# A layer kernel with RWKV-7, band attention and memory attention on one core: the odd chunks of a triangular inverse laid crosswise over TensorE, and three numbers of its planner changed

## The chip, the core and the metric

The kernel runs on one core of a Trainium2 chip. The metric is the device time of one execution in microseconds. A change of less than 0.2% (5.4 us) is about what a measurement of this kernel cannot tell from no change.

TensorE (PE in the profile) multiplies, VectorE (DVE) and ScalarE (ACT) do the elementwise work and empty PSUM, GpSimd (POOL) makes a reduction over partitions for each weight tile, and SyncE (SP) issues the DMA transfers. A weight load of TensorE stands as PEld.

## The reference

Two layers over 512 tokens with 1024 channels. Each layer is a half-step FFN, a mixing block with three branches, and a second half-step FFN:

```python
x = x + 0.5 * swiglu(rms_norm(x, norm_ffn1[l]), ffn1_w_in[l], ffn1_w_out[l])
h = rms_norm(x, norm_mix[l])
proj = h @ w_in[l]            # RWKV | band attention | memory attention
y_rwkv, y_att, y_mem = rwkv7_time_mix(...), chunked_rel_attention(...), memory_attention(...)
merged = g_rwkv * (y_rwkv @ w_branch_rwkv[l]) + g_att * (y_att @ w_branch_att[l]) + g_mem * (y_mem @ w_branch_mem[l])
x = x + merged @ w_out[l]
x = x + 0.5 * swiglu(rms_norm(x, norm_ffn2[l]), ffn2_w_in[l], ffn2_w_out[l])
```

The part that is changed is in the RWKV branch, a scan over time with 8 heads of 64 channels:

```python
def step(state, inp):
    r_t, w_t, k_t, v_t, kk_t, b_t = inp
    sa = jnp.einsum('bhvk,bhk->bhv', state, kk_t)
    state = state * w_t[:, :, None, :] - sa[..., None] * b_t[:, :, None, :] + v_t[..., None] * k_t[:, :, None, :]
    return state, jnp.einsum('bhvk,bhk->bhv', state, r_t)
```

## The kernel before

**Two kinds of products.** The large products (FFN, projections, gates, branches, output) run in fp16: every weight tile comes from HBM as float32 (`wr`), is split by ACT and DVE into a high and a low half (`wh`), and each product is three fp16 products of 128 rows by 128 columns by 512 tokens (`hh`, `hl`, `ab`, `ya`, `ym`, `yr` against `wh`; tiles `g` and `as` in PSUM). RWKV and the two attentions compute in float32 with small products.

**The scan in chunks.** The 512 steps are cut into 8 chunks of 64. `rwkv` runs over four pairs `p` of heads; the two heads of a pair lie on partitions 0 to 63 and 64 to 127 (`H2`; `W2` is the same pair the other way round). For each pair it makes decays and scaled keys (`ar`, `be`, `ka`), then per half of the chunks one block of 16 products `be` and `ka` against `ar`, 64 by 64 by 128 (the "be/ka blocks" below): `be` goes from a head's partitions to the other head's columns, `ka` to its own, so the four 64 by 64 quarters of TensorE are all used. DVE masks the result into `gx` and `g1`.

**The inverse.** The unit lower triangular 64 by 64 matrix of each chunk and head is inverted by doubling. `lab` holds the matrix, `tt` the transposed inverse so far, `ti` the inverse so far. Level 0 needs no product. Levels 1 to 4 (`for n in range(1, 5)`) each take a mask product on DVE (`lm`), a block of 16 products `lm` by `tt` (`each`; rows `s<-tt,ta` in the trace), a copy of it to `p1` (tile `ka`) on ACT, a second block of 16 products `ti` by `p1` (rows `s<-ka,ti`), a subtraction from `tt` on DVE, and four transposes with four copies that refresh `ti` (`turned`, `placed`; the list `PL` says S or V for each copy). There are 2 layers x 4 pairs x 4 levels x 2 = 64 such blocks. A last level works on 32 by 32 pieces. In `each` before, head 0 goes from rows 0 to 63 to columns 0 to 63 and head 1 from rows 64 to 127 to columns 64 to 127: two of the four quarters are used. A float32 product stands in the trace as two instructions, so a block of 16 has 32.

**After the inverse** the 8 chunks go one after the other: `xps`, `cx`, `vu`, the state `vz`, and the output `yp`.

**What sets the order.** No engine's order is written by hand. `Plan` records every operation with its dependencies; a block (`plan.block()`) is one operation of TensorE. `run` then builds a list schedule with costs in us (`cost`, `GROUPS`, `HOPS`), and each engine issues in the order of that plan (every instruction has the line of the replay, L560 before and L562 after). An operation's priority is its `tail`, the longest path behind it, plus a `lift`. Four rules of `run` matter here:

- `GROUPS` gives the cost of a block by number and shape of its products. Where it has no entry, the costs of the single products are added: a be/ka block is then 16 x (0.0255 + 128 / 1200) = 2.1 us.
- `RATIO, DEBT`: each float32 operation adds 0.45 of its cost to a debt, each fp16 operation takes its cost off. Where the debt is over `DEBT`, a float32 operation that would be next has to let an fp16 product go first.
- A pool's tile of a tag waits until all users of the tile that had the buffer are done. Tag `s` in PSUM has two buffers, tag `ta` in SBUF has one.
- `WARM`: where TensorE would wait for over 0.4 us in the plan, the wait is filled with products of a zero tile (`xps<-wt`, 320 columns), which nothing uses.

The fp16 products that can stand between the small ones are the projections (until all are made) and then gates and branches; a gate may run ahead of its branch by two tiles only.

Of the kernel before, what the change touches and what calls it, by code (L numbers as in the profile page):

```python
# [10 lines left out]
AF = mybir.ActivationFunctionType  # L11
ALU = mybir.AluOpType
# [4 lines left out]
P = 128  # L17
# [12 lines left out]
EXPC = 0.6065306597126334  # L30
SPREAD = 3
FIRSTS = ("x00", "pv0", "con", "x01", "w1")
LIFT = 110
PCS = [[0], [1, 2, 3]]
FIRST = 2
# [192 lines left out]
class Plan:  # L228
# [1 line left out]
    GROUPS = {  # L230
        2: {(128, CH, CH): 0.266, (CH, CH, CH): 0.264, **{(CH, P, n): 0.212 + n * 0.001656 for n in (128, 256, 384, 512)}},
        4: {(128, CH, CH): 0.5},
        16: {(CH, CH, CH): 1.08},
    }
    HOPS = {"PE": (0.2, 0.2), "S": (0.14, 0.27), "V": (0.14, 0.21), "G": (0.06, 0.3), "D": (0.5, 0.5)}
    SLACK = 0.04
    RATIO, DEBT = 0.45, 0.5

    def __init__(self, tc):
        nc = tc.nc  # L240
# [337 lines left out]
def trunk(tc: tile.TileContext, i: dict, out: bass.AP, dbg: dict | None = None, depth: int = DEPTH):  # L578
# [32 lines left out]
    def as_stream(name, f, *a):  # L611
        old, stream[0] = stream[0], name
        r = f(*a)
        stream[0] = old
        return r
# [10 lines left out]
    def s_ps():  # L626
        return pq.tile([P, T], F32, tag="s", name=nm("s"))
# [290 lines left out]
    def chunk(src, k=KT):  # L918
        w, d = load_w(src, src.shape[-1])
        return w.rearrange("p s (k n) -> p s k n", k=k), d  # L920
# [72 lines left out]
    def mixing(l, pieces, kst):  # L993
# [43 lines left out]
        def project():  # L1037
            lw = tr("lw")
            D.dma_start(out=lw, in_=i["lora"][l, 0])
            gw = tr("gw")  # L1040
            D.dma_start(out=gw, in_=i["lora"][l, 1])
            w, d = chunk(i["w_in"][l, 0])
            dd = mul_d(d, d_h)
            ps = [g_ps(), g_ps()]
            for c0, c1 in HV:
                mm3x2([x[:, c0:c1] for x in ps], [([(w[:, 0, k, u * P:(u + 1) * P], w[:, 1, k, u * P:(u + 1) * P]) for u in range(2)], hh[:, k, c0:c1], hl[:, k, c0:c1]) for k in range(KT)])
            plan.phase += 1
            xwa = shift(ps[0], dd, 12, "xwa")
            S.activation(xwa[0:CH, :], xwa[0:CH, :], AF.Tanh)
            xg = shift(ps[1], dd, 13, "xg")  # L1050
            S.activation(xg, xg, AF.Tanh, scale=0.5)
            V.tensor_scalar(out=xg, in0=xg, scalar1=0.5, scalar2=0.5, op0=ALU.mult, op1=ALU.add)
            glob.update(lw=lw, gw=gw, xwa=xwa, xg=xg)
            if l > 0:
                va, dva = chunk(i["vres_a"])
                vb = tr("vb", [32, T])
                D.dma_start(out=vb, in_=i["vres_b"])
                ps = g_ps()
                mm3(ps[0:32, :], [(va[:, 0, k, :], va[:, 1, k, :], hh[:, k, :], hl[:, k, :]) for k in range(KT)])
                dv = mul_d(dva, d_h)  # L1060
                hv = tm("yr", bufs=5)[0:32, :]
                S.activation(hv, ps[0:32, :], AF.Copy, scale=dv[0:32, 0:1])
                glob.update(vb=vb, hv=hv)
            for x, p in PLAN:
                if x == "rkv":
                    w, d = chunk(i["w_in"][l, 1 + p])
                    dd = mul_d(d, d_h)
                    r_ = shift(lin(w, d, 0, hh, hl), dd, p, "r")
                    k_ = shift(lin(w, d, 1, hh, hl), dd, 4 + p, "k")
                    w, d = chunk(i["w_v"][l, p])  # L1070
                    rkv_of[p] = r_, k_, shift(lin(w, d, 0, hh, hl), mul_d(d, d_h), 8 + p, "v")
                elif x == "att":
                    w, d = chunk(i["w_av"][l, p])
                    dd = mul_d(d, d_h)
                    ps = g_ps()
                    for b in range(4):
                        mm3(ps[:, b * P:(b + 1) * P], [(hh[:, k, b * P:(b + 1) * P], hl[:, k, b * P:(b + 1) * P], w[:, 0, k, :], w[:, 1, k, :]) for k in range(KT)])
                    vt = ta_("vt", [P, 4, P], bufs=2)
                    S.activation(vt, ps.rearrange("p (b n) -> p b n", b=4), AF.Copy, scale=dd[:, 0:1])
                    V.tensor_reduce(out=vm[:, p:p + 1], in_=vt, op=ALU.max, axis=AX.XY, apply_absolute_value=True)  # L1080
                    w, d = chunk(i["w_in"][l, 5 + p])
                    dd = mul_d(d, d_h)
                    qk = []
                    for u in range(2):
                        t = ta_("ak" if u else "aq", bufs=2)
                        S.activation(t, lin(w, d, u, hh, hl), AF.Copy, scale=dd[:, 0:1])
                        qk.append(t)
                    att_of[p] = qk[0], qk[1], vt
                else:
                    w, d = chunk(i["w_in"][l, 9 + p])  # L1090
                    dd = mul_d(d, d_h)
                    for u in range(2):
                        t = ta_("ak" if u else "aq", bufs=2)
                        S.activation(t, lin(w, d, u, hh, hl), AF.Copy, scale=dd[:, 0:1])
                        mq_of[2 * p + u] = t
# [3 lines left out]

        def band():  # L1100
            for p in range(NP):
                q_, k_, vt = att_of[p]
                bias = ta_("bias", [P, 2, 2 * P])
                D.dma_start(out=bias, in_=i["bias"][l, p])
# [77 lines left out]
        def mem_att():  # L1182
            for c in range(2):
                for u in range(2):
                    j = 2 * c + u
                    q_ = mq_of[j]
                    sq = ta_("sc", bufs=3)
                    S.activation(sq, q_, AF.Square)
# [42 lines left out]
        def c8(t):  # L1231
            return t.rearrange("p (c s) -> p c s", c=NCH)

        def lev(c0, n=NCH):
            return con[:, c0:c0 + CH].unsqueeze(1).to_broadcast([P, n, CH])

        def each(ps, f, to=H2):
            with plan.block():
                for c in range(NCH):
                    for h, o in zip(H2, to):  # L1240
                        a, b = f(h, c)
                        PE.matmul(ps[o, c * CH:(c + 1) * CH], lhsT=a, rhs=b, start=True, stop=True)

        def turned(src):

            ps = s_ps()
            with plan.block():
                for b in range(4):
                    PE.transpose(ps[:, b * P:(b + 1) * P], src[:, b * P:(b + 1) * P], ident)
            return ps.rearrange("p (b h a) -> p b h a", b=4, h=2)  # L1250

        def placed(ps, dst, engines):

            for n, (r, h) in enumerate(((0, 0), (1, 1), (0, 1), (1, 0))):
                o = dst(h).rearrange("p (b r) a -> p b r a", r=2)[:, :, r, :]
                if engines[n] == "S":
                    S.activation(o, ps[H2[r], :, h, :], AF.Copy)
                else:
                    V.tensor_copy(o, ps[H2[r], :, h, :])
# [2 lines left out]

        def rwkv():
            for p in range(NP):
                cs = slice(p * P, (p + 1) * P)
                r_, k_, v_ = rkv_of[p]

# [75 lines left out]
                placed(turned(ut.rearrange("p c s -> p (c s)")), lambda h: lab[H2[h]], PL[20:24])  # L1343
                V.tensor_tensor(out=tt, in0=ut, in1=lev(C_LEV1T), op=ALU.mult)
                V.tensor_tensor(out=tt, in0=lev(C_EYE), in1=tt, op=ALU.subtract)
                ti = tr("ti", [P, NCH, CH])
                V.tensor_tensor(out=ti, in0=lab, in1=lev(C_LEV), op=ALU.mult)
                V.tensor_tensor(out=ti, in0=lev(C_EYE), in1=ti, op=ALU.subtract)
                aw = small("aw", 8)
                for u, h in enumerate(H2):  # L1350
                    o, x = gx[W2[u], :, u, :], ar[h].rearrange("p c a s -> p c (a s)")
# [14 lines left out]
                for n in range(1, 5):  # L1366
                    lm = tr("ta", [P, NCH, CH])
                    V.tensor_tensor(out=lm, in0=lab, in1=lev(C_LEV + n * CH), op=ALU.mult)
                    ps = s_ps()
                    each(ps, lambda h, c: (lm[h, c, :], tt[h, c, :]))  # L1370
                    p1 = tr("ka", [P, NCH, CH])
                    S.activation(p1, c8(ps), AF.Copy)
                    pt = s_ps()
                    each(pt, lambda h, c: (ti[h, c, :], p1[h, c, :]))
                    V.tensor_tensor(out=tt, in0=tt, in1=c8(pt), op=ALU.subtract)
                    placed(turned(tt.rearrange("p c s -> p (c s)")), lambda h: ti[H2[h]], PL[16:20])

                up, low = [[slice(CH * h + b, CH * h + b + CH // 2) for h in range(2)] for b in (0, CH // 2)]
                lo, hi = slice(0, CH // 2), slice(CH // 2, CH)
# [95 lines left out]

        def branch(b, y):
            for m in range(4):
                w, d = chunk(i["w_gate"][l, b * 4 + m])
                dg = mul_d(d, d_h, 0.5)
                bw, bd = chunk(i["w_branch"][l, b, m], k=4)  # L1480
# [21 lines left out]
                        S.activation(sq, acc[n], AF.Square, accum_out=qm[:, n:n + 1])  # L1502

        as_stream("f", project)
        plan.lift = LIFT
        as_stream("m", rwkv)
        plan.lift = 0.0
        as_stream("a", band)
        as_stream("a", mem_att)
        tst.close()  # L1510
        gp = tst.enter_context(plan.pool(name=nm("gp"), bufs=1, reuse_waits="tile"))
        acc.extend(gp.tile([P, T], F32, name=nm("acc")) for _ in range(4))
# [3 lines left out]
        for b, y in ((1, ya), (2, ym), (0, yr)):  # L1516
            wide[0] = b != 1
            as_stream("f", branch, b, y)
        plan.step(False)
        dump(f"acc{l}", acc[0])  # L1520

# [182 lines left out]
```

## Time and profile before

| | |
|---|---|
| median of 3 runs | 2720.83 us (2719.52 to 2721.28) |
| profiled execution | 2720.14 us |
| its span, first to last instruction | 2718.4 us |
| busy | PE 2682.8, PEld 1458.5, DVE 1623.0, ACT 1534.9, POOL 111.9 us |
| mean granted clock of TensorE | 0.997 |
| read from HBM | 239.09 MB, 91 GB/s with the writes over the span |

The trace falls into five stretches: the first FFN (0 to 400 us), the mixing of layer 0 (400 to 884), two FFNs (884 to 1768), the mixing of layer 1 (1768 to 2244), and the last FFN. RWKV, the attentions and everything that the change touches lie in the two mixing stretches.

How to read the rows: a timeline row has the start in us from the span's start, the length in us, the engine, the line, the operation, the tiles written and read, the array's shape (`64*64`), the size and the number of instructions merged; in brackets the idle time of the engine before it and what ended it. A matmul's own length includes its way through the array, so what it costs is the distance to the next start. A row of a stretch gives per engine the busy us and in brackets the instructions, and then TensorE's granted clock, the DMA share and GB/s. A row of a group gives the count, and behind the bar the busy us, the mean ns of one, and the idle us before them.

### The profile page before, as it was taken

Reading aid. Unit: us, or ns where it says so; the run is one execution under the profiler, and the core shown is the slowest. Engines: PE = TensorE matmul, PEld = TensorE weight load, DVE = VectorE, ACT = ScalarE, POOL = GpSimd, SP = SyncE. Lnnn points to the kernel's source line nnn. Section 1 sums busy time; section 2 is a strip of 40 time slices with the busy share of each in tenths; the row PEclk is TensorE's granted clock in tenths of the full one; section 3 lists DMA queues with packets and bytes.
Section 4 is the critical chain, followed back from the end, with each engine's and each line's share of the span. In section 5 each row is a group of like instructions: output and inputs, shape, how many; then the busy total and the mean of one; then the engine's idle time right before and its main releaser. Section 6 shows DMA issues by size and latency. Waiting matters only on the chain.

```text
span 2718.4 us, 45525 instructions
## 1 busy us (share of the span) xinstructions
PE 2682.8 (99%) x18206; PEld 1458.5 (54%) x18206; DVE 1623.0 (60%) x4391; ACT 1534.9 (56%) x2543; POOL 111.9 (4%) x285
## 2 busy tenths in 40 slices
PE   9999999999999999999999999999999999999999
PEld 6444486565645465444564444765645454654445
DVE  6345487788676675354463444777876756743543
ACT  6556465665545666565455654665655546655652
POOL 0000000000000000000000000000000000000000
PEclk9999999999999999999999999999999999999999
DMA  5222342121121223222222223311102213223232
GB/s 172 102 100 105 113 144 75 63 71 36 47 86 71 93 94 118 108 99 97 99 109 99 104 101 124 120 68 59 63 28 78 74 48 113 94 105 106 96 109 78
DMA packets 47158, 249.37 MB, mean 92 GB/s; under 512 B 5312, under 2 KB 10688, under 8 KB 23648
## 3 DMA queue, kind: packets, MB, share of 16 engines
q1 hardware_dynamic: 46944, 246.45, 25.6%
q8 instruction: 143, 2.34, 0.3%
q14 instruction: 71, 0.58, 0.1%
HBM read 239.09 MB, written 7.34 MB: 91 GB/s over the span
## 4 chain that ended last, share of the span: by engine, by line
PE 87%; DVE 8%; ACT 2%; issue 1%; DMA 0%; POOL 0%; SPq 0%; ACTq 0%; POOLq 0%; DVEq 0%
PE g L560 45%; PE as L560 33%; PE s L560 5%; PE xps L560 3%; DVE wh L560 1%; DVE w L560 1%; PE yp L560 1%; DVE gx L560 1%; DVE rs L560 1%; DVE sc L560 1%; ACT wh L560 0%; DVE ar L560 0%; ACT pt L560 0%; DVE tt L560 0%; DVE be L560 0%
## 5 line engine op out<-in xcount | busy, mean ns | idle before, releaser
L560 PEld LDWEIGHTS <-wh 128*128 128x128 f16 x10920 | 1049.8, 98 | 1017.0 <-issue 31.6
L560 PE MATMUL g<-hh,wh 128*128 128x512 f16 (+1 forms) x3216 | 984.2, 367 | 3.0 <-DVE r L560 2.1
L560 ACT ACTIVATE wh<-wr,qs 128x1024 f16<-128x1024 f32 (+2 forms) x478 | 482.9, 1050 | 222.4 <-PE g L560 120.4
L560 ACT ACTIVATE junk<-wr 128x2048 uint8<-128x2048 f32 (+2 forms) x239 | 413.0, 1728 | 333.3 <-DMA wr<-ffn_in 142.4
L560 PE MATMUL g<-hl,wh 128*128 128x512 f16 (+1 forms) x1608 | 589.2, 366 | 0.0
L560 DVE SCALAR_TENSOR_TENSOR wh<-wr,qs,wh 128x1024 f16<-128x1024 f32 (+2 forms) x478 | 544.4, 1169 | 48.6 <-ACT wh L560 47.7
L560 PE MATMUL as<-hh,wh 128*128 128x512 f16 (+1 forms) x1536 | 443.4, 361 | 0.0
L560 PE MATMUL as<-hl,wh 128*128 128x512 f16 (+1 forms) x768 | 277.4, 361 | 0.0
L560 PE MATMUL as<-ab,wh 128*128 128x512 f16 (+1 forms) x1224 | 234.7, 350 | 0.0
L560 PE MATMUL g<-ab,wh 128*128 128x512 f16 (+1 forms) x1224 | 234.5, 350 | 0.0
L560 POOL PARTITION_ALL_REDUCE ar<-wm x239 | 97.4, 408 | 2391.9 <-ACT junk L560 2171.0
L560 DVE SCALAR_TENSOR_TENSOR a<-g,md,sg 128x512 f32<-128x512 f32 x44 | 33.0, 751 | 213.5 <-PE g L560 209.3
L560 DVE SCALAR_TENSOR_TENSOR a<-as,md,sg 128x512 f32<-128x512 f32 x44 | 33.0, 751 | 213.3 <-PE as L560 210.1
L560 DVE SCALAR_TENSOR_TENSOR x<-g,md,x 128x512 f32<-128x512 f32 (+1 forms) x62 | 39.0, 629 | 116.2 <-PE g L560 116.1
L560 DVE SCALAR_TENSOR_TENSOR x<-as,md,x 128x512 f32<-128x512 f32 (+1 forms) x62 | 39.0, 629 | 114.6 <-PE as L560 114.6
L560 DVE TENSOR_SCALAR qt<-ar 128x1 int32<-128x1 int32 x253 | 37.9, 151 | 103.1 <-POOL ar L560 100.8
L560 ACT ACTIVATE sq<-x 128x256 f32<-128x256 f32 x96 | 37.0, 407 | 79.5 <-DVE x L560 51.9
L560 PE MATMUL xps<-wt 128*128 128x320 f16 x390 | 64.0, 312 | 5.1 <-DVE ta L560 3.8
L560 DVE SCALAR_TENSOR_TENSOR ab<-a,qs,ab 128x512 f16<-128x512 f32 x88 | 60.7, 747 | 9.6 <-ACT ab L560 9.3
L560 ACT ACTIVATE ti<-s 64x256 f32<-64x256 f32 (+1 forms) x144 | 54.3, 377 | 17.9 <-PE s L560 15.0
L560 ACT ACTIVATE sg<-as,md 128x512 f32<-128x512 f32 x44 | 30.1, 685 | 56.3 <-PE as L560 56.2
L560 ACT ACTIVATE sg<-g,md 128x512 f32<-128x512 f32 x44 | 30.1, 684 | 55.0 <-PE g L560 54.9
(345 smaller groups left out, 3060.8 us busy)
## 6 DMA issues: line engine op xcount, KB each, us to landing
wr<-ffn_in SPq DMA_DIRECT2D x88, 1024.0 KB, 4.8
wr<-ffn_outa SPq DMA_DIRECT2D x32, 1024.0 KB, 4.8
wr<-w_gate SPq DMA_DIRECT2D x24, 1024.0 KB, 4.9
wr<-w_in SPq DMA_DIRECT2D x22, 1024.0 KB, 4.8
wr<-ffn_outb SPq DMA_DIRECT2D x16, 768.0 KB, 4.4
wr<-w_branch SPq DMA_DIRECT2D x24, 512.0 KB, 3.7
wr<-mem_kv SPq DMA_DIRECT2D x8, 1024.0 KB, 4.9
wr<-w_out SPq DMA_DIRECT2D x8, 1024.0 KB, 4.8
```

Of the source, the lines that this page charges most:

```text
L560: f(*[x.real() if isinstance(x, View) else x for x in a], **{y: x.real() if isinstance(x, View) else x for y, x in k.items()})
```

## The change

`each` now sends odd chunks crosswise: the product of head 0 goes from rows 0 to 63 to columns 64 to 127, and that of head 1 the other way. Even chunks write one PSUM tile and odd chunks a second one, so a block holds both buffers of `s`. In the second block the way is turned back, which needs `ti` with its heads swapped in odd chunks: level 0 makes it so with three DVE operations out of a new tile `low` (tag `ta`), and `placed` does it with `cross` on levels 1 to 3. The copy to `p1` is split (even chunks on ACT, odd chunks on DVE), and the subtraction from `tt` is two DVE operations in place of one.

In the planner, the block of 16 of 64 by 64 by 64 costs 0.63 us in place of 1.08, be/ka blocks and the 32 by 32 blocks get entries of their own (1.04 and 0.625), and `DEBT` goes from 0.5 to 2.0. A table `LIFTS` of priorities per operation is read in several places; it is empty, so that all lifts stay as before (110 for `rwkv`, 0 elsewhere).

```diff
@@ class Plan
-        16: {(CH, CH, CH): 1.08},
+        16: {(CH, CH, CH): 0.63, (CH, CH, P): 1.04, (CH // 2, CH // 2, CH // 2): 0.625},
...
-    RATIO, DEBT = 0.45, 0.5
+    RATIO, DEBT = 0.45, 2.0
@@ mixing
-        def each(ps, f, to=H2):
+        def each(f, back):
+            pss = [s_ps(), s_ps()]
             with plan.block():
                 for c in range(NCH):
-                    for h, o in zip(H2, to):
-                        a, b = f(h, c)
-                        PE.matmul(ps[o, c * CH:(c + 1) * CH], lhsT=a, rhs=b, start=True, stop=True)
+                    r = c % 2
+                    for u in range(2):
+                        x = u ^ r
+                        a, b = f(H2[x if back else u], c)
+                        PE.matmul(pss[r][H2[u if back else x], c // 2 * CH:(c // 2 + 1) * CH], lhsT=a, rhs=b, start=True, stop=True)
+            return [p[:, 0:T // 2].rearrange("p (b a) -> p b a", b=NCH // 2) for p in pss]
+
+        def parity(t, r):
+            return t.rearrange("p (b r) a -> p b r a", r=2)[:, :, r, :]
...
-        def placed(ps, dst, engines):
+        def placed(ps, dst, engines, cross=False):
             for n, (r, h) in enumerate(((0, 0), (1, 1), (0, 1), (1, 0))):
-                o = dst(h).rearrange("p (b r) a -> p b r a", r=2)[:, :, r, :]
+                o = dst(h ^ r if cross else h).rearrange("p (b r) a -> p b r a", r=2)[:, :, r, :]
@@ rwkv
+                low = tr("ta", [P, NCH, CH])
+                V.tensor_tensor(out=low, in0=lab, in1=lev(C_LEV), op=ALU.mult)
                 ti = tr("ti", [P, NCH, CH])
-                V.tensor_tensor(out=ti, in0=lab, in1=lev(C_LEV), op=ALU.mult)
-                V.tensor_tensor(out=ti, in0=lev(C_EYE), in1=ti, op=ALU.subtract)
+                for r, (a, b) in ((0, (slice(0, P), slice(0, P))), (1, H2), (1, H2[::-1])):
+                    o, x = parity(ti[a], r), parity(low[b], r)
+                    V.tensor_tensor(out=o, in0=lev(C_EYE, 4)[b], in1=x, op=ALU.subtract)
...
                 for n in range(1, 5):
                     lm = tr("ta", [P, NCH, CH])
                     V.tensor_tensor(out=lm, in0=lab, in1=lev(C_LEV + n * CH), op=ALU.mult)
-                    ps = s_ps()
-                    each(ps, lambda h, c: (lm[h, c, :], tt[h, c, :]))
+                    pss = each(lambda h, c: (lm[h, c, :], tt[h, c, :]), False)
                     p1 = tr("ka", [P, NCH, CH])
-                    S.activation(p1, c8(ps), AF.Copy)
-                    pt = s_ps()
-                    each(pt, lambda h, c: (ti[h, c, :], p1[h, c, :]))
-                    V.tensor_tensor(out=tt, in0=tt, in1=c8(pt), op=ALU.subtract)
-                    placed(turned(tt.rearrange("p c s -> p (c s)")), lambda h: ti[H2[h]], PL[16:20])
+                    S.activation(parity(p1, 0), pss[0], AF.Copy)
+                    V.tensor_copy(parity(p1, 1), pss[1])
+                    for r, pt in enumerate(each(lambda h, c: (ti[h, c, :], p1[h, c, :]), True)):
+                        V.tensor_tensor(out=parity(tt, r), in0=parity(tt, r), in1=pt, op=ALU.subtract)
+                    placed(turned(tt.rearrange("p c s -> p (c s)")), lambda h: ti[H2[h]], PL[16:20], n < 4)
```

**What moves.** All the products are the same in number. SP's loads keep their places but for six of 306 (three `bias`, one `mx`, and one pair of `w_in` and `w_v` that changes places). On TensorE the fp16 products are followed by a float32 product 402 times in place of 424, and the array's shape changes 741 times in place of 765. The `xps<-wt` products go from 390 to 423: 5 more in the mixing of layer 0 (68 to 73) and 28 more in that of layer 1 (22 to 50). DVE has 80 instructions more, ACT as many as before.

The first place is on TensorE, in the mixing of layer 0, where the second pair of heads goes through its chunks (`xps`, `yp`) beside the band attention (`as<-pt,vt` is its last product for a pair of heads; rows of the same block that follow are left out). Before:

```order
L560 MATMUL xps<-cx_7197,tt_5689 64x64 x2
L560 LDWEIGHTS wh_6742
L560 MATMUL g_7088<-hh_2569,wh_6742 128x512
...
L560 MATMUL as_7323<-pt_6811,vt_5931 64x512
...
L560 LDWEIGHTS wh_6742
L560 MATMUL g_7088<-hh_2569,wh_6742 128x512
...
L560 MATMUL xps<-kk_6860,kb_1103_5666 64x64
L560 MATMUL xps<-ta_6724,be_6317 64x64
L560 LDWEIGHTS wh_7072
...
L560 MATMUL yp_5764<-ar_6263,gx_5719 64x64 x2
```

On TensorE at the same place after:

```order
L562 MATMUL xps<-cx_7209,tt_5821 64x64 x2
L562 MATMUL as_7322<-con,sc_7214 128x2 x4
L562 MATMUL as_7309<-pt_6574,vt_5811 64x512
...
L562 MATMUL xps<-kk_7009,kb_1113_5774 64x64
L562 MATMUL xps<-ta_6935,be_6396 64x64
L562 MATMUL yp_5896<-ar_6345,gx_5849 64x64 x2
L562 MATMUL yp_5896<-kk_7009,g_1100_5850 64x64
L562 MATMUL yp_5896<-ta_6935,g_1100_5850 64x64
L562 LDWEIGHTS wh_6868
```

The three runs of fp16 products between the small blocks are gone; they come behind the last of them.

The second place is on DVE, in the first pair of layer 0, where the two be/ka blocks are masked into `gx` and `g1` (names `gx`, `g`), with the split of a weight tile (`wh`) in between. Before:

```order
L560 TENSOR_TENSOR gx_4122<-s_4619,con 64x4x128 x2
L560 TENSOR_TENSOR g_1002_4123<-s_4512,con 128x256
L560 SCALAR_TENSOR_TENSOR wh_4662<-wr_4495,qs_4290,wh_4662 128x1024 x2
L560 TENSOR_SCALAR qt_4464<-ar_4265 128x1
...
L560 TENSOR_TENSOR gx_4122<-s_4725,con 64x4x128 x2
L560 TENSOR_TENSOR g_1002_4123<-s_4724,con 128x256
L560 TENSOR_TENSOR tt_4121<-ti_4120,con 128x512
```

On DVE at the same place after:

```order
L562 TENSOR_TENSOR gx_4122<-s_4619,con 64x4x128 x2
L562 TENSOR_TENSOR g_1002_4123<-s_4512,con 128x256
...
L562 SCALAR_TENSOR_TENSOR wh_4662<-wr_4495,qs_4290,wh_4662 128x1024
L562 TENSOR_TENSOR g_1002_4123<-s_4713,con 128x256
L562 TENSOR_TENSOR gx_4122<-s_4714,con 64x4x128 x2
L562 TENSOR_TENSOR tt_4121<-ti_4120,con 128x512
...
L562 COPY cx_4116<-xps 128x64
L562 SCALAR_TENSOR_TENSOR wh_4662<-wr_4495,qs_4290,wh_4662 128x1024
```

The second half of the weight split now stands behind the masks of both blocks, and behind the first copy of the chunk chain (`cx`) too.

The third place is on TensorE, in the last pair of layer 0, ahead of the first block of the inverse (`s<-tt,ta`). Before:

```order
L560 MATMUL s_9343<-con,v_8044 128x128 x4
...
L560 LDWEIGHTS wh_9141
L560 MATMUL g_9266<-ya_7374,wh_9141 128x512
L560 MATMUL s_9371<-w_9103,con 128x512
L560 MATMUL s_9378<-tt_8894,ta_9200 64x64 x16
L560 MATMUL xps<-ar_9289,gx_8907 64x64 x2
```

On TensorE at the same place after (18 products of the zero tile stand there):

```order
L562 MATMUL s_9396<-con,v_8096 128x128 x4
L562 MATMUL s_9405<-w_9152,con 128x512
L562 MATMUL xps<-ar_9335,gx_8979 64x64 x2
L562 LDWEIGHTS wt
L562 MATMUL xps<-wt 128x320
...
L562 MATMUL s_9422<-tt_8955,ta_9413 64x64 x2
L562 MATMUL s_9423<-tt_8955,ta_9413 64x64 x2
```

The fp16 products that covered the way to the first block are gone from there, a planned wait stands in their place, and the block alternates between two PSUM tiles.

More of the change, by code (lines that the diff above doesn't have):

```diff
@@ L32 @@
 FIRSTS = ("x00", "pv0", "con", "x01", "w1")
+LIFTS = {}
 LIFT = 110
@@ L1064, in project @@
             for x, p in PLAN:
+                plan.lift = LIFTS.get((x, l, p), 0.0)
                 if x == "rkv":
@@ L1101, in band @@
             for p in range(NP):
+                plan.lift = LIFTS.get(("b", l, p), 0.0)
                 q_, k_, vt = att_of[p]
@@ L1185, in mem_att @@
                     j = 2 * c + u
+                    plan.lift = LIFTS.get(("m", l, j), 0.0)
                     q_ = mq_of[j]
@@ L1264, in rwkv @@
             for p in range(NP):
+                plan.lift = LIFTS.get(("r", l, p), LIFT)
                 cs = slice(p * P, (p + 1) * P)
@@ L1477, in branch @@
             for m in range(4):
+                plan.lift = LIFTS.get(("g", l, b, m), 0.0)
                 w, d = chunk(i["w_gate"][l, b * 4 + m])
@@ L1504, in mixing @@
         as_stream("f", project)
-        plan.lift = LIFT
+        plan.lift = 0.0
         as_stream("m", rwkv)
@@ L1509, in mixing @@
         as_stream("a", mem_att)
+        plan.lift = 0.0
         tst.close()
@@ L1518, in mixing @@
             as_stream("f", branch, b, y)
+        plan.lift = 0.0
         plan.step(False)
```

## Prediction

> **What bounds the kernel now.** I read the page first, then the stretches, then the groups by shape, then the order of time on TensorE. From the page, its span, the first row of the engines and the chain that ended last:
>
> ```profile
> span 2718.4 us, 45525 instructions
> PE 2682.8 (99%) x18206; PEld 1458.5 (54%) x18206; DVE 1623.0 (60%) x4391; ACT 1534.9 (56%) x2543; POOL 111.9 (4%) x285
> PE 87%; DVE 8%; ACT 2%; issue 1%; DMA 0%; POOL 0%; SPq 0%; ACTq 0%; POOLq 0%; DVEq 0%
> ```
>
> TensorE is busy 99% of the span and holds 87% of the chain. What is taken off its queue comes off the time, if the waits do not grow. The two mixing stretches, by stretch (PE, PEld, DVE, ACT, POOL busy, clock):
>
> ```profile
> 400.00:884.00 484.00, 472.50 (x4464) 273.72 (x4463) 357.57 (x1127) 274.73 (x580) 17.20 (x43) 1.00 0.18 65
> 1768.00:2244.00 476.00, 460.76 (x4321) 260.79 (x4320) 350.95 (x1062) 268.45 (x571) 15.31 (x39) 0.99 0.17 60
> ```
>
> Idle there: 484.0 - 472.5 + 476.0 - 460.8 = 26.7 us of 960. DVE is busy 708.5 of 960, 74%. So in both TensorE's queue sets the time and the float32 chain keeps up.
>
> **The crosswise blocks.** The groups of the two blocks, by shape, with the zero products:
>
> ```profile
> L560 PE MATMUL s<-ka,ti 64*64 64x64 f32 x1024 | 37.1, 221 | 2.0 <-ACT ka L560 2.0
> L560 PE MATMUL s<-tt,ta 64*64 64x64 f32 x1024 | 36.7, 221 | 0.1
> L560 PE MATMUL xps<-wt 128*128 128x320 f16 x390 | 64.0, 312 | 5.1 <-DVE ta L560 3.8 <-DVE wt L560 1.0 <-DVE ar L560 0.3
> ```
>
> 2048 instructions, 32 in a block: 64 blocks. What one costs is the distance between starts, from TensorE's order of time:
>
> ```profile
> 453.09 0.38 PE L560 MATMUL g<-hl,wh 128*128 128x512 f16 x1
> 453.31 0.38 PE L560 MATMUL g<-hh,wh 128*128 128x512 f16 x1
> 453.62 1.15 PE L560 MATMUL s<-ka,ti 64*64 64x64 f32 x32
> 454.70 0.39 PE L560 MATMUL g<-hh,wh 128*128 128x512 f16 x1
> ```
>
> 454.70 - 453.62 = 1.08 us for a straight block of 32 instructions, 16 in each of its two quarters. No block in the trace is crosswise with 64 columns, but the be/ka blocks use all four quarters with 128 columns:
>
> ```profile
> 434.49 0.33 PE L560 MATMUL s<-ar,be 64*64 64x128 f32 x2
> 434.50 0.33 PE L560 MATMUL s<-ar,ka 64*64 64x128 f32 x2
> 434.65 0.28 PE L560 MATMUL s<-ar,be 64*64 64x128 f32 x2
> 434.67 0.28 PE L560 MATMUL s<-ar,ka 64*64 64x128 f32 x2
> 434.76 0.28 PE L560 MATMUL s<-ar,be 64*64 64x128 f32 x2
> ...
> 435.31 0.28 PE L560 MATMUL s<-ar,be 64*64 64x128 f32 x2
> 435.32 0.28 PE L560 MATMUL s<-ar,ka 64*64 64x128 f32 x2
> 435.53 0.39 PE L560 MATMUL g<-hh,wh 128*128 128x512 f16 x1
> ```
>
> Eight steps of four instructions, 0.11 apart (434.65 to 434.76; 434.65 to 435.31 is six of them): 0.87 of the 435.53 - 434.49 = 1.04 us, the other 0.17 is the way in and out. The straight block then has (1.08 - 0.17) / 16 = 0.057 for a step of 64 columns, half of 0.11. Crosswise, 8 steps x 0.057 + 0.17 = 0.63 us. That asks for an instruction each 0.46 / 32 = 0.014 us; the 32 by 32 blocks have that pace already:
>
> ```profile
> 475.64 0.69 PE L560 MATMUL s<-tt,kk 32*32 32x32 f32 x32
> 476.26 0.39 PE L560 MATMUL g<-hh,wh 128*128 128x512 f16 x1
> ```
>
> (476.26 - 475.64 - 0.17) / 32 = 0.014. The diff's own costs for these two blocks, 1.04 and 0.625, are what the rows give, so its 0.63 may be a measurement too; I lean on the rows. Term: 64 x (1.08 - 0.63) = **-28.8 us**. Ends: 0, if two quarters of the same rows do not overlap with other data, and -28.8; I take the second, being nearest to the be/ka rows.
>
> A rule speaks against it. The Trainium skill, "TensorE: Matmul & The Clock Gate", section "Part 3: Packing small matmuls — row/col tiling", says that a weight load overlaps with products in flight only if its row group is another one. By that, the loads of the two quarters in the same rows would wait for each other's products, the block would stay near 1.08, and the term would be 0. In this trace, weight loads of the be/ka block:
>
> ```profile
> 434.55 0.14 PEld L560 LDWEIGHTS s<-ar,be 64*64 64x64 f32 x2
> 434.56 0.14 PEld L560 LDWEIGHTS s<-ar,ka 64*64 64x64 f32 x2
> ```
>
> They start at 434.55 and 434.56, while the first products of the same rows run from 434.49 to 434.83. So the rows decide against the rule.
>
> **DEBT.** The order has 424 - 402 = 22 passages fewer from fp16 to float32, and 765 - 741 = 24 changes of the array's shape fewer. A change costs 453.62 - 453.31 less the 0.22 of an fp16 product (453.09 to 453.31) = 0.09 us. Term: 24 x 0.09 = **-2.2 us**, from 0 to twice that. "Four times" in the debt is thus little in the order. Less cover between dependent float32 blocks is its price; that is the wait term below.
>
> **Zero products.** 33 more x 64.0 / 390 = 0.164 us = **+5.4 us**. They stand where the planner sees a wait, so they replace idle time if the wait is real and add time if it is not; as they cannot be left out, I count them whole. From 0 to 5.4.
>
> **VectorE and ScalarE.** Groups by shape, copies and sums of the inverse:
>
> ```profile
> L560 DVE COPY kk<-s 64x256 f32<-64x256 f32 x16 | 6.8, 427 | 2.5 <-ACT kk L560 1.9
> L560 DVE TENSOR_TENSOR tt<-tt,s 128x512 f32<-128x512 f32 x32 | 21.9, 683 | 24.9 <-PE s L560 24.8
> L560 ACT ACTIVATE ka<-s 128x512 f32<-128x512 f32 x32 | 19.1, 596 | 46.9 <-PE s L560 46.7
> L560 ACT ACTIVATE ti<-s 64x256 f32<-64x256 f32 x128 | 48.3, 377 | 6.1 <-PE s L560 3.2 <-DVE rs L560 0.6
> ```
>
> DVE: 32 new copies of 256 (0.43 each) 13.7; 64 half subtractions at 0.43 for 32 at 0.68, +5.5; at level 0 three of 256 for one of 512, 8 x (1.28 - 0.68) = +4.8. Together +24 us, from 74% to (708.5 + 24) / 930 = 79% of the mixing: beside TensorE's queue, so 0 on the path. ACT: 32 x (0.60 - 0.38) = 7 us less, 0 on the path. On the chain of the inverse a level loses 2 x 0.45 in products and 0.60 - 0.43 in the copy, and gains 0.86 - 0.68 in the subtraction: 0.9 us shorter. Ahead of the first block, `lm` must wait until `low`, in the same buffer, is written and read: 0.69 + 3 x 0.43 = 2.0 us more. Over a pair, 4 x 0.9 - 2.0 = 1.6 us shorter. The cover of all this is fp16 products; where it is gone (third place of the order) TensorE waits for it, the second rival.
>
> **Waits.** TensorE's waits: the two that end in DVE's work on the be/ka blocks, and that for a weight split:
>
> ```profile
> PE s L560 <- DVE kk L560: 4.2, 5, 1.3
> PE s L560 <- DVE gx L560: 4.0, 7, 0.8
> ...
> PE g L560 <- DVE wh L560: 0.4, 1, 0.4
> ```
>
> One of each, in TensorE's and DVE's order of time:
>
> ```profile
> 443.01 0.63 PE L560 MATMUL s<-con,ti 128*128 128x128 f32 x4 [0.77 <-DVE gx L560]
> 446.51 0.63 PE L560 MATMUL s<-con,ka 128*128 128x128 f32 x4 [1.14 <-DVE kk L560]
> 438.32 2.47 DVE L560 SCALAR_TENSOR_TENSOR wh<-wr,qs,wh 128x1024 f16<-128x1024 f32 x2
> 441.48 1.39 DVE L560 TENSOR_TENSOR gx<-s,con 64x512 f32<-64x512 f32 x2
> ```
>
> The planner held a be/ka block for 2.1 us where it takes 1.04, so TensorE came early and stood: `gx` had both halves of `wh` ahead of it. After, one half of 1.24 us is behind, and fp16 products stand between the transposes. What is late instead is that half: the fp16 products of this weight tile wait for it, 0.4 us in all before, with room to grow. Of the 8.2 us I take half, **-4 us**; the ends are -8.2 and +15.6 (the 2.0 us of the second rival on all 8 pairs). I am nearer to the gain because a planned wait is already counted at +5.4.
>
> **Sum**, against the profiled execution's own 2720.1 us (0.7 under the median shown): -28.8 - 2.2 + 5.4 - 4 = -29.6, so 2690.5; I say **2690**.
>
> **Rivals.**
>
> 1. *The crosswise block is no faster*: for it the rule above, against it the be/ka rows. Then -2.2 + 5.4 - 4 = -0.8 and 2719, no change. Chance 4%.
> 2. *Half of the gain turns into waits.* The way to the first block is 2.0 us longer, and at three of the eight such places the fp16 products run out in the new order (10, 18 and 22 zero products where none stood); with fewer of them between float32 blocks, DVE at 79% shows. Price 8 x 2.0 = 16 us: 2706. For it: all three rows of waits above end in DVE. Against: only 26.7 us of idle time in 960 now. Chance 22%.
> 3. *Slower, by the clock.* Longer stretches of small float32 products and waits let TensorE's clock fall. Three stretches where fp16 products had run out:
>
> ```profile
> 648.00:690.00 42.00, 38.59 (x307) 23.22 (x305) 38.97 (x112) 24.19 (x70) 1.12 (x3) 1.00 0.04 14
> 1972.00:2040.00 68.00, 63.68 (x457) 33.03 (x455) 55.38 (x173) 37.73 (x90) 1.06 (x4) 0.97 0.10 32
> 2060.00:2108.00 48.00, 43.76 (x417) 27.05 (x416) 25.04 (x76) 23.57 (x53) 0.39 (x1) 0.93 0.22 78
> ```
>
> In the last two it fell already: 68 x 0.03 + 48 x 0.07 = 5.4 us lost. It turns the gain round if 29.6 us more are lost in the 960: a mean of (960 - 35) / 960 = 0.96 decides. A mean of 0.8 on some 270 us (612 to 748 and 1972 to 2108) costs 54, 49 more than now: 2739. Against it, 648 to 690, where the old order has 46 zero products (7.5 us) and float32 of two branches around them, kept 1.00. Chance 5%. The Trainium skill has this in "TensorE: Matmul & The Clock Gate", "Part 1: The HAM clock gate (the "warmup" mystery)": a window with too little work halves the clock. The two later stretches agree with that; the first shows a stretch of this kind that does not.
> 4. *More gain*: all 8.2 us of waits go, and the 5.4 us of clock: 2681. Chance 9%.
>
> **How the numbers follow.** The forecast has 60%. Its own range is 2686 to 2699, the waits between -8.2 and +4. With the second and fourth rival it is 2679 to 2709, which leaves out 9%, and some misses in size. Faster: 60 + 22 + 9 = 91%; same 4%; slower 5%.
>
> **What would show it.** Blocks `s<-tt,ta` and `s<-ka,ti` with starts 0.63 apart from the next product; the two groups at about 37 us in sum in place of 74; both mixing stretches shorter, by some 16 us (layer 0, 5 zero products more) and 13 us (layer 1, 28 more); the waits on DVE `gx` and `kk` under 8.2 us; the other three stretches as before. I am wrong if a block is over 0.8 us, if the idle time in the mixing is over 40 us, or if the clock there is under 0.98.

## The result and the profile after

The changed kernel takes 2692.7 us (median) against 2721.1 before: ratio 0.9897, 95% interval 0.9881 to 0.9912. The forecast was 2690, and the measured time lies in its range. The sum came out in part by luck: the blocks brought less than their term, and the rest of the change more.

The page after, its span and the first row of the engines:

```profile
span 2693.6 us, 45695 instructions
PE 2664.2 (99%) x18239; PEld 1440.6 (53%) x18239; DVE 1639.0 (61%) x4471; ACT 1528.3 (57%) x2543; POOL 109.2 (4%) x285
```

The span is 24.8 us shorter, TensorE's busy time 18.6. Its order of time at one crosswise block after, the block and the next product:

```profile
452.52 0.69 PE L562 MATMUL s<-tt,ta 64*64 64x64 f32 x32
453.15 0.39 PE L562 MATMUL g<-hh,wh 128*128 128x512 f16 x1
```

453.15 - 452.52 = 0.63 us, as worked out from the be/ka blocks. The groups after, of the two products of the inverse, the zero products, and the new forms on DVE and ACT:

```profile
L562 PE MATMUL xps<-wt 128*128 128x320 f16 x423 | 70.5, 316 | 5.5 <-DVE cx L562 3.1 <-ACT kk L562 1.4 <-DVE wt L562 1.0
L562 PE MATMUL s<-tt,ta 64*64 64x64 f32 x1024 | 25.0, 225 | 0.6 <-ACT ti L562 0.4
L562 DVE TENSOR_TENSOR tt<-tt,s 128x256 f32<-128x256 f32 x64 | 24.0, 414 | 5.2 <-PE s L562 5.0
L562 PE MATMUL s<-ka,ti 64*64 64x64 f32 x1024 | 22.3, 224 | 0.1
L562 DVE COPY ka<-s 128x256 f32<-128x256 f32 x32 | 13.5, 421 | 11.3 <-PE s L562 10.9
L562 ACT ACTIVATE ka<-s 128x256 f32<-128x256 f32 x32 | 12.2, 382 | 20.2 <-PE s L562 14.9 <-ACT ti L562 4.0 <-issue 1.0
```

The two product groups fall from 73.8 to 47.3 us of busy time, which includes the way through the array of a block's last product. Where the span went, by two rows of the order of time, before and then after: the first product of layer 1's first pair (`xwa,lw`) and the norm of the last FFN (`con,na`):

```profile
1775.00 1.13 PE L560 MATMUL s<-xwa,lw 64*128 64x512 f32 x4
2356.64 0.50 PE L560 MATMUL s<-con,na 128*128 128x1 f32 x4
```

```profile
1766.76 1.13 PE L562 MATMUL s<-xwa,lw 64*128 64x512 f32 x4
2330.85 0.58 PE L562 MATMUL s<-con,na 128*128 128x1 f32 x4 [0.48 <-DVE qt L562]
```

Up to the first pair of layer 1 8.2 us are gained, up to the last FFN 25.8: 8 us in the mixing of layer 0 and 18 in that of layer 1. The last FFN gives 1.0 us back.

For all kernels below, one measure is read from each page and its group of zero products: TensorE's wait, that is the span less PE's busy time, plus the busy time of the zero products. Before: 2718.4 - 2682.8 + 64.0 = 99.6 us. After: 2693.6 - 2664.2 + 70.5 = 99.9. So the waits in all are as they were, and the gain is in PE's other busy time, 2618.8 before and 2593.7 after. That rest is not the products alone. A matmul's record includes its way in and out, so a short wait between two products can hide in it, and so does a lower clock. In this execution the stretches at a granted clock of 0.50 ahead of the last products add up to 27.3 us, in the one before to 13.7.

### The profile page after: what moved, and what is told of

Read it like the earlier page. It is cut to its first block, busy times and chain, and to the rows that moved or that the text cites. A ratio compares the mean times of both kernels' runs of the same rounds, so it can differ in the third digit from the quotient of the medians.

```text
span 2693.6 us, 45695 instructions
## 1 busy us (share of the span) xinstructions
PE 2664.2 (99%) x18239; PEld 1440.6 (53%) x18239; DVE 1639.0 (61%) x4471; ACT 1528.3 (57%) x2543; POOL 109.2 (4%) x285
## 5 line engine op out<-in xcount | busy, mean ns | idle before, releaser
L562 ACT ACTIVATE ti<-s 64x256 f32<-64x256 f32 (+1 forms) x144 | 54.3, 377 | 63.4 <-PE s L562 47.3
L562 PE MATMUL xps<-wt 128*128 128x320 f16 x423 | 70.5, 316 | 5.5 <-DVE cx L562 3.1
L562 ACT ACTIVATE sg<-as,md 128x512 f32<-128x512 f32 x44 | 30.1, 683 | 56.3 <-PE as L562 56.2
```

What stands on the lines that cost most here:

```text
L562: f(*[x.real() if isinstance(x, View) else x for x in a], **{y: x.real() if isinstance(x, View) else x for y, x in k.items()})
```

## The experiments

All stand against the kernel before on the same chip. The time is the median of all executions; the columns behind the ratio are of the profiled one. "Zero" is the busy time of the zero products, the clock is the mean granted clock. PE idle includes the 4 us or so ahead of the first product, which the idle times in the expectations leave out (31.5 us there is 35.6 here). The kernel before took 2719.9 to 2721.1 us beside the different runs.

| kernel | time us | ratio (95%) | PE idle | zero | wait | clock |
|---|---|---|---|---|---|---|
| before | 2721.1 | | 35.6 | 64.0 | 99.6 | 0.997 |
| after | 2692.7 | 0.9897 (0.9881 to 0.9912) | 29.4 | 70.5 | 99.9 | 0.995 |
| after, blocks straight (e4) | 2715.5 | 0.998 (0.9971 to 0.9989) | 27.6 | 70.5 | 98.1 | 0.995 |
| before + costs + DEBT 2.0 (e3) | 2702.6 | 0.9934 (0.9922 to 0.9947) | 20.0 | 59.9 | 79.9 | 0.997 |
| before + costs (e5) | 2721.9 | 1.0004 (0.9995 to 1.0013) | 32.2 | 68.7 | 100.9 | 0.997 |
| before + DEBT 2.0 (e6) | 2712.0 | 0.9973 (0.9963 to 0.9983) | 36.2 | 56.2 | 92.4 | 0.997 |
| crosswise alone (e12) | 2729.0 | 1.0031 (1.0019 to 1.0042) | 43.3 | 90.8 | 134.1 | 0.998 |
| crosswise + DEBT 2.0 (e2) | 2732.2 | 1.004 (1.0027 to 1.0052) | 55.2 | 59.4 | 114.6 | 0.994 |
| crosswise + costs (e1) | 2709.0 | 0.9961 (0.9949 to 0.9974) | 27.4 | 90.9 | 118.3 | 0.998 |
| after, block's cost 1.08 (e8) | 2707.9 | 0.996 (0.9947 to 0.9972) | 33.7 | 72.4 | 106.1 | 0.997 |
| after, `low` elsewhere (e7) | 2700.3 | 0.993 (0.9918 to 0.9943) | 41.8 | 63.6 | 105.4 | 0.995 |
| after, lift 115 (e11) | 2712.0 | 0.9968 (0.9956 to 0.998) | 36.5 | 73.9 | 110.4 | 0.992 |
| `low` elsewhere, DEBT 4.0 (e10) | 2686.3 | 0.9878 (0.9864 to 0.9891) | 28.3 | 68.3 | 96.6 | 0.998 |
| `low` elsewhere, lift 105 (e9) | 2680.8 | 0.9856 (0.9842 to 0.9869) | 21.8 | 72.6 | 94.4 | 0.998 |

### Straight blocks in the order of the changed kernel

```diff
 # each
-                        x = u ^ r
-                        a, b = f(H2[x if back else u], c)
-                        PE.matmul(pss[r][H2[u if back else x], ...], lhsT=a, rhs=b, start=True, stop=True)
+                        a, b = f(H2[u], c)
+                        PE.matmul(pss[r][H2[u], ...], lhsT=a, rhs=b, start=True, stop=True)
 # level 0: ti out of low with no heads swapped; placed: dst(h) without the swap
 # the planner still charges the 0.11 us of a swap, so that the order stays the same
```

> The changed kernel with the odd chunks sent straight again (two of the four quarters of TensorE), everything else kept: two PSUM tiles, the split copy and subtraction, the planner's numbers, and the same order on every engine, instruction by instruction. Theory A (the crosswise blocks carry the gain): a block goes from 0.63 back to 1.08 us, 64 x 0.45 = 28.8 us more than the changed kernel's 2692.7, so 2717 to 2722. Rival B (the new order carries it, and the blocks are covered anyway): 2693 to 2698. Rival C (half of the blocks' time is hidden behind waits of the chain): about 2707.

Measured 2715.5 (2712.2 to 2720.6). The groups of this kernel:

```profile
L562 PE MATMUL s<-tt,ta 64*64 64x64 f32 x1024 | 38.1, 222 | 0.2 <-ACT ti L562 0.2
L562 PE MATMUL s<-ka,ti 64*64 64x64 f32 x1024 | 36.7, 221 | 0.0
```

and its page:

```profile
span 2717.4 us, 45695 instructions
PE 2689.8 (99%) x18239; PEld 1467.7 (54%) x18239; DVE 1641.7 (60%) x4471; ACT 1528.2 (56%) x2543; POOL 109.6 (4%) x285
```

74.8 us in place of 47.3, with the same order on every engine, costs 22.8 us. Theory A holds nearly: 22.8 of 28.8, and a time 1.5 us under its range. PE's busy time without zero products is 25.6 us longer and the wait 1.8 shorter (98.1 for 99.9). The order of the changed kernel, with the straight blocks it was not made for, is 5.4 us faster than before, about the least that can be told from no change.

### The planner's part alone

```diff
-        16: {(CH, CH, CH): 1.08},
+        16: {(CH, CH, CH): 1.08, (CH, CH, P): 1.04, (CH // 2, CH // 2, CH // 2): 0.625},
-    RATIO, DEBT = 0.45, 0.5
+    RATIO, DEBT = 0.45, 2.0
```

> The kernel before with the planner's part of the change alone: costs of 1.04 for be/ka blocks and 0.625 for the 32 by 32 blocks (the straight blocks keep 1.08, which is what they take), DEBT 2.0. Its order has 376 zero products and 749 changes of shape, against 390 and 765 before. Theory A: 14 x 0.164 + 16 x 0.09 = 3.7 us less, and up to 8 us of waits on DVE gx and kk: 2709 to 2718 against 2721 before. Rival B: the order carries half of the gain or more: 2707 or less.

Measured 2702.6, the rival's number: 18.3 us without one product made shorter. Its page:

```profile
span 2699.5 us, 45509 instructions
PE 2679.5 (99%) x18192; PEld 1461.0 (54%) x18192; DVE 1623.6 (60%) x4391; ACT 1533.4 (57%) x2543; POOL 111.0 (4%) x285
```

The wait is 2699.5 - 2679.5 + 59.9 = 79.9 us, 19.7 less than before. The gain is all wait. My prediction had 4 us for the waits and 2.2 for `DEBT`.

Its two halves, `GROUPS` alone and `DEBT` alone:

> The kernel before with the planner's costs of the be/ka blocks (1.04 for 2.1) and of the 32 by 32 blocks (0.625) alone; straight blocks at 1.08, DEBT 0.5. The two planner changes together gave 2702.6 from 2720.9. Its order has 420 zero products (390 before) and 762 changes of shape (765). Theory F (a right cost of the be/ka blocks takes away the waits of TensorE, idle time 31.5 to 16.4 us in the two together): 30 x 0.164 = 4.9 us more and some 15 less: 2706 to 2714. Rival G (DEBT carries it): 2718 to 2727.

> The kernel before with DEBT 2.0 alone, all costs as before. Its order has 350 zero products (390 before) and 742 changes of shape (765). Theory F (the costs carry the planner's gain): 40 x 0.164 + 23 x 0.09 = 8.7 us less at most, and as much again in waits that now stand bare: 2712 to 2722, idle time of TensorE at 31 us or more. Rival G (DEBT carries it): 2701 to 2708, idle time under 20 us.

The costs alone change nothing (2721.9, as rival G said; the interval holds 1). The debt alone gives 8 us less (2712.0, at the edge of theory F's range), and the two together 18. So neither the costs nor the debt carries it alone: with these orders it takes both. Waits of TensorE on DVE `gx` and `kk`, 8.2 us before, went to 2.4 with the costs alone (`kk` only), to 5.7 with the debt alone and to 2.0 with both (`kk` only). These rows thus have at most 6.2 of the 18 us; the rest is spread over many rows.

### The crosswise blocks without the planner's part

```diff
 # the changed kernel with
+        16: {(CH, CH, CH): 1.08},
+    RATIO, DEBT = 0.45, 0.5     # e12; e2 keeps 2.0
```

> The crosswise blocks alone: the changed kernel with the planner's old costs (1.08 for a block that takes 0.63, 2.1 for be/ka blocks) and DEBT 0.5. With the old costs and DEBT 2.0 it was 2732, with the new costs and DEBT 0.5 it was 2709. Its order has 559 zero products. Theory J (a planner that holds the blocks for longer than they take gives the gain back in waits): 2715 to 2735, idle time and zero products together over 110 us. Rival A (shorter blocks on a busy TensorE come off the time by themselves): 2692 to 2700.

> The changed kernel with the old costs of blocks in the planner (1.08 for the blocks of 64, 2.1 for the be/ka blocks), crosswise blocks and DEBT 2.0 kept. Its order has 368 zero products and 736 changes of shape. Theory A: the blocks take 0.63 whatever the planner believes, so the time stays within 2684 to 2697: 55 zero products less are worth between 0 and 9 us. Rival E (the measured costs are needed, since TensorE otherwise comes early and stands at the be/ka blocks as it did before): 2700 to 2710, with waits of TensorE on DVE gx and kk at 8 us again.

2729.0 and 2732.2: with the blocks made 0.45 us shorter and the planner not told, the kernel is slower than before. The page of the first:

```profile
span 2727.8 us, 45995 instructions
PE 2684.5 (98%) x18375; PEld 1449.5 (53%) x18375; DVE 1640.9 (60%) x4471; ACT 1527.8 (56%) x2543; POOL 110.5 (4%) x285
```

and the group of its zero products:

```profile
L562 PE MATMUL xps<-wt 128*128 128x320 f16 x559 | 90.8, 308 | 8.2 <-DVE cx L562 3.3 <-DVE ta L562 2.0 <-ACT kk L562 1.5
```

Its wait is 134.1 us, 34.5 more than before: more than all the work saved, as theory J had it. The second has 114.6 and a lower clock, and its time is above both ranges that I gave. I had expected TensorE to stand at the be/ka blocks again, which the waits on `gx` and `kk` would show; in e2 TensorE's waits on these two are 0.5 and 0.7 us:

```profile
PE s L562 <- DVE kk L562: 0.7, 3, 0.2
PE s L562 <- DVE gx L562: 0.5, 2, 0.3
```

The waits of the weight loads of the second (crosswise, DEBT 2.0, old costs), of the kernel before and of the changed one, each with its sum, its count and the longest in us:

```profile
PEld s L562 <- DVE tt L562: 14.0, 26, 1.2
PEld s L562 <- ACT ka L562: 9.1, 16, 1.0
```

```profile
PEld s L560 <- ACT ka L560: 2.5, 1, 2.5
PEld s L560 <- DVE tt L560: 2.4, 5, 0.6
```

```profile
PEld s L562 <- ACT ka L562: 3.5, 9, 0.6
PEld s L562 <- DVE tt L562: 2.2, 7, 0.5
```

The weight loads of the second block of a level wait for the copy `ka`, those of the transposes and of the last level for the subtraction `tt`: 4.9 us before, 23.1 here, 5.7 in the changed kernel. One such place in e2, TensorE first and then DVE:

```profile
455.16 0.69 PE L562 MATMUL s<-ka,ti 64*64 64x64 f32 x32
456.88 0.38 PE L562 MATMUL g<-hh,wh 128*128 128x512 f16 x1
457.44 0.66 PE L562 MATMUL s<-con,tt 128*128 128x128 f32 x4 [0.19 <-DVE tt L562]
455.97 0.75 DVE L562 SCALAR_TENSOR_TENSOR wh<-wr,qs,wh 128x512 f16<-128x512 f32 x1 [0.37 <-ACT wh L562]
456.64 0.74 DVE L562 TENSOR_TENSOR tt<-tt,s 128x256 f32<-128x256 f32 x2
```

The block's last product ends at 455.85, but DVE has half a weight split ahead of the subtraction, which starts at 456.64. A plan that holds a block for 1.08 us has room for that split; the real block is done earlier, and the transposes wait. Counted in the traces over the 32 second blocks, the subtraction starts over 0.3 us after the block's end in 25 of them in e2, 24 in e12 and 12 in the changed kernel. The number of fp16 products between the two blocks of a level is not the reason: it is 201 in all in e2 and 186 in the changed kernel.

The block's cost alone, put back:

```diff
-        16: {(CH, CH, CH): 0.63, (CH, CH, P): 1.04, ...},
+        16: {(CH, CH, CH): 1.08, (CH, CH, P): 1.04, ...},
```

> The changed kernel with the planner's cost of a crosswise block left at 1.08 (it takes 0.63), be/ka blocks at 1.04 and DEBT 2.0 kept. Its order has 456 zero products and 732 changes of shape. With both costs old the time was 2732. Theory J (the wrong cost of the 64 crosswise blocks makes the order late on DVE and ACT and uncovers the chain): 2715 to 2732, with TensorE idle for 40 us or more. Rival K (the be/ka cost is what was missing): 33 x 0.166 - 9 x 0.09 = 4.7 us more than the changed kernel at most: 2692 to 2698.

2707.9, between the two expectations: 15.2 us over the changed kernel, with idle time of only 33.7 us. Weight loads and TensorE itself on the same two tiles:

```profile
PEld s L562 <- DVE tt L562: 13.5, 20, 4.0
PEld s L562 <- ACT ka L562: 7.5, 14, 1.0
```

```profile
PE s L562 <- DVE tt L562: 5.7, 6, 3.5
PE s L562 <- ACT ka L562: 1.1, 4, 0.5
```

The weight loads wait 21.0 us in place of 5.7, and the subtraction is over 0.3 us late at 27 of the 32 blocks. These 15.3 us are not simply the loss, though the numbers agree: of TensorE's own idle time the two tiles have 6.8 us. Between the two profiled executions, 11.6 us apart, the wait grew by 6.2 us (99.9 to 106.1) and PE's other busy time by 5.4. The other costs, be/ka's among them, have the rest, 2732.2 - 2707.9 = 24 us. So the block's cost and the others both count once the blocks are short.

### DEBT in the changed kernel

```diff
-    RATIO, DEBT = 0.45, 2.0
+    RATIO, DEBT = 0.45, 0.5
```

> The changed kernel with DEBT back at 0.5. Its order has 574 zero products in place of 423, 756 changes of shape in place of 741, and 424 passages from fp16 to float32 in place of 402. Theory A' (DEBT is worth its changes of shape only, 15 x 0.09 = 1.4 us, and the zero products only fill waits that are there in both): 2693 to 2697. Rival D (with the small debt the fp16 products are used up early, and the chain then stands bare, which the zero products show: 151 x 0.165 = 25 us): 2710 to 2720.

2709.0, 16.3 us slower. The zero products take 90.9 us in place of 70.5, the idle time is 27.4: the rival D, in its direction and nearly in its size. My term for DEBT was 2.2 us of changes of shape; the run speaks for rival D's account, that the larger debt keeps fp16 products for later, but no run isolates it from the chance of an order (see the next section).

### The buffer of low, and neighbours of the order

```diff
-                low = tr("ta", [P, NCH, CH])
+                low = tr("w", [P, NCH, CH], bufs=3)
```

> The changed kernel with the tile low in a buffer of tag w (three buffers, one of them free there) in place of the one that the next mask product lm needs. Its order has 389 zero products in place of 423 and 723 changes of shape in place of 741. Theory H (the wait of lm for low, 2.0 us at each of 8 places, is paid where the fp16 products run out): 34 x 0.166 + 18 x 0.09 = 7.3 us less: 2683 to 2688 against 2692.7. Rival I (the zero products only fill time in which TensorE would wait for something else): 2690 to 2695.

2700.3: 34 zero products less and 7.6 us slower. Both theories miss. The wait is 105.4 us, 5.5 more than in the changed kernel: zero products take 6.9 us less, and the idle time is 12.4 us longer (41.8 for 29.4).

A wait taken away that makes the kernel slower speaks for the order, not for the buffer. Three more kernels test that: the same buffer with the order chosen anew (lift 105, or DEBT 4.0), and the changed kernel with lift 115.

```diff
 # e9: low in tag w, and
-LIFT = 110
+LIFT = 105
 # e10: low in tag w, and DEBT = 4.0
 # e11: the changed kernel, and LIFT = 115
```

> The changed kernel with the lift of rwkv at 115 in place of 110 and nothing else: no work is added or taken away, the priorities move a little. Its order has 444 zero products and 743 changes of shape (423 and 741). Theory L (a list schedule's neighbours scatter by several us): 2698 to 2710, all of it in idle time and zero products. Rival N (such a step does nothing): 2690 to 2696.

> The changed kernel with low in a buffer of tag w, and the lift of rwkv at 105 in place of 110. Its order has 445 zero products (423 in the changed kernel, 389 with low in tag w at lift 110, which was 7.6 us slower). Theory L (the time of one list schedule against its neighbours is partly chance, so the buffer has to be judged with the order chosen anew; the planner's own sum is lowest here): 2680 to 2691. Rival M (the buffer itself does harm, or the zero products show the waits): 2696 to 2704.

> The changed kernel with low in a buffer of tag w and DEBT 4.0, lift 110. Its order has 424 zero products, 378 passages from fp16 to float32 and 724 changes of shape, against 423, 402 and 741. Theory L: 2682 to 2694 with the idle time of TensorE near 26 us again. Rival M (the buffer does harm): 2696 to 2704, idle time near 38 us as with DEBT 2.0.

Lift 115 adds no work and costs 19.3 us (2712.0), 2 us over the range of theory L. And the loss is not all in idle time and zero products: the wait is 110.4, 10.5 more than in the changed kernel, but PE's other busy time grew too, by 8.2 us, at a clock of 0.992. With the buffer the other two take 2680.8 and 2686.3, within theory L's ranges, so the buffer does no harm that a new order does not outweigh.

This scatter is a rival for every comparison of two orders above that differs by less than 20 us: e1, e3, e5, e6 and e8 are one order each. For the costs the traces speak beyond it: the subtraction is over 0.3 us late at 24 to 27 of 32 blocks in the three crosswise kernels planned with 1.08, and at 9 to 13 in the six planned with 0.63. For `DEBT` no row separates the kernels like that. Only e4, with the order held, is free of it.

The best kernel is e9, ratio 0.9856 (0.9842 to 0.9869) against before and 11.9 us under the changed one. Its page:

```profile
span 2677.8 us, 45777 instructions
PE 2656.0 (99%) x18261; PEld 1437.3 (54%) x18261; DVE 1637.9 (61%) x4471; ACT 1529.6 (57%) x2543; POOL 111.7 (4%) x285
```

and the group of its zero products:

```profile
L562 PE MATMUL xps<-wt 128*128 128x320 f16 x445 | 72.6, 310 | 3.5 <-DVE ta L562 2.1 <-DVE wt L562 1.0 <-DVE cx L562 0.4
```

More zero products than after, and the least idle time of all crosswise kernels: 21.8 us. Of the 15.8 us between the spans of the two profiled executions, 5.5 are wait. The other 10.3 are PE's other busy time, and of the products nothing was taken away; the clock was 0.998 here and 0.995 there.

## Why the prediction was right, and where it was not

- **Crosswise blocks, -28.8.** The mechanism is shown: 0.63 us for a block after, 1.08 in the straight kernel with the same order. The size was 22.8 on the path. Their PE busy time less zero products differs by (2689.8 - 70.5) - (2664.2 - 70.5) = 25.6 us, and the changed kernel waits 1.8 more. The two groups fell to 47.3 us, not to the 37 that I named as a sign: a block's row is 0.69 us long in place of 1.15, since the way in and out does not halve with it. The rule of the Trainium skill, "TensorE: Matmul & The Clock Gate", "Part 3: Packing small matmuls — row/col tiling", that a weight load overlaps only with products of another row group, disagrees with the 0.63 us measured, since by it the block would have stayed near 1.08.
- **All the rest, -0.8 in sum (-2.2, +5.4, -4).** With the order held at the changed kernel's, e4 puts it at -5.4: 6.0 us too much for the blocks and 4.6 too little for the rest. That these two nearly cancel is luck.
- **The planner's costs and DEBT, -2.2 and -4.** These two terms had the wrong mechanism. I took DEBT as changes of shape and the costs as half of the waits on `gx` and `kk`. With straight blocks the two bring 18.3 us (e3), of which those waits are at most 6.2, and with crosswise blocks 36.3 (2729.0 of e12 less 2692.7).
- **The terms do not add up one by one.** I added the blocks to the planner's terms as if each had its price in any order. The crosswise blocks are worth 22.8 us in the changed kernel's order, and 9.9 against e3, where the planner's part has its 18.3 already. The wait is 79.9 us in e3 and 99.9 after. The shorter blocks alone are not what bares these 20 us, for with straight blocks in the same order e4 waits 98.1. They come with the order that was planned for the crosswise kernel; which of its parts makes them (the cost of 0.63, both buffers of `s` in one block, `low`, or the chance of one order) stays open.
- **Zero products, +5.4.** They took 6.5 us more (64.0 to 70.5), but to count them as added time was wrong in kind: e7 lost 34 of them and got slower, and e9 has more of them and is the fastest. Mostly they mark waits that are there.
- **The waits on gx and kk, -4.** 8.2 to 1.9 us, these two after:

```profile
PE xps L562 <- DVE cx L562: 3.1, 2, 1.8
PE s L562 <- DVE be L562: 2.4, 3, 1.0
...
PE s L562 <- DVE kk L562: 1.2, 3, 0.6
...
PE s L562 <- DVE gx L562: 0.7, 1, 0.7
```

  More than I took, and others (`cx`, `be`) stand in their place: PE's idle time fell by 6.2 us in all.
- **DVE +24, ACT -7.** Busy time +16.0 and -6.6. The copies took 0.42 us each as priced (13.5 in all) and the subtractions 24.0 in place of 21.9, where I had +5.5. Both lay beside the queue, as said; DVE is 61% of the span.
- **The stages.** I gave 16 us to layer 0 and 13 to layer 1; it was 8 and 18. Of the signs of being wrong none came: a block takes 0.63 us, the idle time in the mixing is 20 us, and the clock there is 0.99.
- **The low buffer (second rival).** Alone it did not pay; with two new orders it is in the two fastest kernels. What part of e9's 11.9 us is the buffer and what the luck of the order stays open: no kernel with lift 105 and the old buffer was run.
- **The clock (third rival).** It did not turn the result. But it moves it: the changed kernel's four executions took 2689.5 and 2690.2 at 0.997, and 2695.2 and 2695.4 at 0.994 and 0.995. The profile is of one of the latter, so its clock accounts for some of the 24.8 us not being 28.4. An estimate from the half-clock stretches: (27.3 - 13.7) / 2 = 6.8 us more were lost after than before, so that at one clock PE's other busy time would have fallen by some 32 us in place of 25.1.

## What to carry to other kernels

When a list schedule orders the queues, a faster block has to be told to it: the same shorter blocks gave -28 us with right costs and a larger debt, and +9 us without either; with the block's cost alone left wrong, 15 us of the gain were gone, and the trace shows VectorE late behind the blocks. Read a gain from wait (span less busy time, plus filler) and from the other busy time apart, and look at the clock before you call the latter work. To price one part of a change, hold the order, as e4 does. Judge a small change by several neighbouring orders, not by one: here a change of priority by 5 us, with no work in it, moved the time by 19 us.

## What was not expected of the hardware

- Four 64 by 64 quarters of TensorE work at the full pace of each with 64 columns and different data: a block of 32 instructions in 0.63 us, 0.014 us an instruction past the 0.17 us of the way in and out. The forecast had this from rows with 128 columns alone.
- The same program, in the same order, takes times 5 us apart (2690 and 2695), and the mean granted clock goes with them (0.997 and 0.994 to 0.995). e4 shows it too: 2719.2 and 2720.6 at 0.995, 2716.9 and 2717.0 at 0.996, 2712.2 to 2715.8 at 0.997 and over.
- The clock can fall to half right behind a stretch in which the profile has TensorE busy throughout. In the kernel after, the 7.0 us ahead of a half-clock stretch and the stretch itself, then the two longest rows of the first:

```profile
511.10:518.10 7.00, 7.00 (x80) 5.16 (x77) 4.59 (x15) 4.73 (x12) 0.00 (x0) 1.00 0.09 18
518.10:521.50 3.40, 3.40 (x35) 3.28 (x34) 3.17 (x19) 1.19 (x2) 0.00 (x0) 0.50 0.31 122
```

```profile
513.21 2.33 PE L562 MATMUL as<-pt,vt 128*64 128x512 f32 x16
515.73 1.95 PE L562 MATMUL as<-con,sc 128*128 128x2 f32 x16
```

  TensorE had no idle time in these 7.0 us. 16 products of 2 columns stand there for 1.95 us; whether so few columns are what lets the clock fall is not shown.
